# Right sides and split weights at chosen distances modulo 512 bytes, and the last norm's root on ScalarE, in a float32 network of six sub-layers

## The chip, the core and the metric

The kernel runs on one core of a Trainium2 chip. A core has a TensorE (PE, for matrix products, with its weight load shown as PEld), a VectorE (DVE), a ScalarE (ACT), a GpSimd (POOL) and a SyncE (SP, which here only issues DMAs), 128 partitions of on-chip memory that the engines read and write, and eight PSUM banks that PE writes its sums to. The metric is the device time of one execution in microseconds (us); single instructions are told in nanoseconds (ns).

## The reference

One sequence of 256 tokens of width 1024 passes two layers of three sub-layers each, all in float32. Each sub-layer normalises, scales and shifts its input by vectors made from a condition `c`, and adds a gated result to `x`:

```python
h = modulate(x, 0)                      # rms_norm(x) * (1 + scale) + shift
x = x + 0.5 * (1 + gate0) * ((silu(h @ w_gate) * (h @ w_up)) @ w_down)
h = modulate(x, 1)
y = hybrid_mixer(h, ...) if layer % 2 == 0 else mlstm_block(h, ...)
x = x + (1 + gate1) * y
h = modulate(x, 2)
x = x + 0.5 * (1 + gate2) * swiglu(h, ...)
...
return rms_norm(x, final_norm_g)
```

The order is feed-forward, hybrid (a gated linear recurrence beside a state-space mixer), feed-forward, feed-forward, mLSTM, feed-forward: sub-layers 0 to 5. The feed-forward hidden width is 2816, that is 22 blocks of 128. Nearly all work is in the projections, 2,928 weight blocks of 128 x 128.

## The kernel before, in words

**Products in parts.** The kernel keeps activations transposed, channels on partitions and the 256 tokens along the free side. A float32 product is made of three products of the fast type float32r: a number is split into a high part (rounded) and a low part (the rest), and high x high, low of the right side x high weights, and high x low weights are summed. Lines 312 to 314 (`multiply`) are these three matmuls of 256 columns; `project` runs them over the k blocks. In the interleaved starts of sub-layers 1 to 5 (`begin`, lines 359 to 361) four banks are filled in turn by matmuls of 258 columns, the last two columns being the shift. In the out projections of the feed-forward sub-layers and of the mLSTM (`out_project`, lines 413 and 415) the right side's high and low part lie behind each other, so one matmul of 512 columns with the high weights and one of 256 with the low weights do the same: a pair. Eight output chunks `d` of 22 (feed-forward) or 16 (mLSTM) pairs each make an out projection. Its result is added to `x` with the gate by DVE (line 420, once for each of the two sums of a pair), squared by ACT (line 296) and the squares are summed by DVE (line 300) for the next norm.

**Weights.** They come in the order of use, in 366 pieces of eight blocks, 512 KB each: SP's queue loads a piece into one of three raw buffers `wraw`, ACT copies the rounded high part `whi` (line 94), DVE subtracts it to give the low part `wlo` (line 95); each has six buffers. Pieces are made up to four ahead of use. Vectors from `c` (`ada`, line 209) are further loads and DVE operations between the pieces.

**Addresses.** Every tile takes a stretch of each partition, in the order in which the pools hand them out. Modulo 512 bytes the tiles that matmuls read lie as follows. The normalised input `hb` has rows of 640 numbers, the high part at their start and the low part 272 numbers (1,088 bytes) on, at 416 and 480. A part buffer is 1,024 + 16 numbers (4,160 bytes), each 64 further than the one before: the six of `whi` at 416, 480, 32, 96, 160, 224, those of `wlo` at 288, 352, 416, 480, 32, 96. The out projection's right sides are at 480 (`ph` of sub-layers 2 and 5; `ysb` and `ylb` of the hybrid), 0 (`ph` of sub-layers 0 and 3; half of the mLSTM's `yb`) or 32 (its other half), `xlb` of the hybrid at 64; in these the low part is 1,024 bytes behind the high one and so at the same place. Pieces named later lie so: 104 and 110 at 160 (`whi`) and 32 (`wlo`), 116 likewise, 167 at 416 and 480, 168 and 330 at 32 and 288.

**The end.** `rs_tokens` (called at line 1051) sums the squares over channels with four one-column matmuls (line 273, block by block: both summands of the first 128 tokens, then both of the second), and DVE makes the inverse root by a bit trick and three Newton steps (lines 278, 255 to 262; twelve operations). PE transposes `x`, already scaled by ACT with the norm's weights (line 1054), into four banks; ACT and DVE each scale two of 512 columns by the inverse root (lines 1062, 1064) and send each off (line 1065).

The compiler of the language puts the instructions of each engine in order by the data they need; nothing in the source fixes it but a few hints (`issue_after`, `add_manual_dep`).

## Time and profile before

| what | us |
|---|---|
| median of 3 runs (1157.63, 1157.66, 1162.23) | 1157.66 |
| the profiled execution | 1161.48 |
| its span, first to last instruction | 1159.6 |
| PE busy, of the span | 1135.5 |
| DVE busy | 958.6 |
| ACT busy | 640.1 |

The stages, by the first and last matmul of each in us of the span: feed-forward 0 from 22 (its `gu` matmuls) over 143 (out projection) to 204; hybrid to 396; feed-forward 2 to 588, its out projection from 526; feed-forward 3 to 777, its out projection from 714; mLSTM to 960, its out projection from 914; feed-forward 5 to 1151, its out projection from 1087.

A row of the timeline has start, length, engine, line, operation and the tiles that it writes and reads (`gu<-hb,whi`: into bank `gu`, from `hb` with the weights `whi`; buffer numbers are left out), then the shape. A matmul's length is modelled and overlaps the next one, so its pace is read from start to start. `xN` counts instructions. A bracket at the end is the engine's idle time before, and what ended it.

### The profile page before, as it was taken

What the parts mean: (1) busy time and instruction counts of PE and PEld (TensorE: products, weight loads), DVE (VectorE), ACT (ScalarE), POOL (GpSimd) and SP (SyncE); (2) the same over time, 40 slices, a digit from 0 to 9 for tenths busy, and PEclk for the clock granted to TensorE, in tenths of its full rate; (3) what the DMA queues carried; (4) which work ended last, traced back from release to release, by engine and by line L of the source; (5) the groups of instructions that cost most, each with busy time, mean ns of one, the idle gap of its engine ahead of it and who ended that gap; (6) DMA issues with size and microseconds to landing.
All of it is one profiled execution on the core that took longest, in us unless ns stands there. A gap on an engine that the chain in (4) does not pass through costs nothing.

```text
span 1159.6 us, 21861 instructions
## 1 busy us (share of the span) xinstructions
PE 1135.5 (98%) x8526; PEld 1080.9 (93%) x8526; DVE 958.6 (83%) x1838; ACT 640.1 (55%) x1070; POOL 8.8 (1%) x24
## 2 busy tenths in 40 slices
PE   7999999999998999999999999999999999999997
PEld 6999988999988999998899998889999889999986
DVE  7989999999888798788788888989869988666553
ACT  4465444778975564444454445448765366544451
POOL 0000000000000000000000000010000000000000
PEclk9999999999999999999999999999999999999999
DMA  8989989556555659888849799973532475775551
GB/s 321 344 299 362 369 301 323 200 184 203 175 182 164 189 191 325 298 313 301 269 148 323 279 344 346 329 266 99 158 110 73 133 241 157 253 229 188 183 182 37
DMA packets 74985, 272.25 MB, mean 235 GB/s; under 512 B 8417, under 2 KB 8577, under 8 KB 74882
## 3 DMA queue, kind: packets, MB, share of 16 engines
q1 hardware_dynamic: 74016, 268.99, 68.4%
q8 instruction: 67, 1.10, 0.4%
q0 software_dynamic: 432, 1.10, 0.3%
q10 hardware_dynamic: 434, 0.76, 0.2%
q14 instruction: 36, 0.29, 0.1%
HBM read 269.77 MB, written 1.05 MB: 234 GB/s over the span
## 4 chain that ended last, share of the span: by engine, by line
PE 83%; DVE 9%; DMA 4%; ACT 3%; issue 1%; ACTq 0%; DVEq 0%; SPq 0%
PE od L413 16%; PE gu L313 12%; PE gu L312 12%; PE gu L314 12%; PE od L415 8%; DMA wraw<-in_wst_dram 4%; DVE wlo L95 3%; ACT whi L94 1%; PE gu_f L361 1%; PE gu_f L359 1%; PE up L314 1%; PE up L313 1%; PE gu_f L360 1%; PE up L312 1%; DVE ada L209 1%
## 5 line engine op out<-in xcount | busy, mean ns | idle before, releaser
L94 ACT CAST whi<-wraw 128x1024 fp32r<-128x1024 f32 x364 | 380.3, 1047 | 299.0 <-DMA wraw<-in_wst_dram 164.1
L95 DVE TENSOR_TENSOR wlo<-wraw,whi 128x1024 fp32r<-128x1024 f32 x366 | 446.6, 1221 | 103.2 <-ACT whi L94 102.4
L313 PE MATMUL gu<-hb,whi 128*128 128x256 f32 x1312 | 369.3, 282 | 0.1
L314 PE MATMUL gu<-hb,wlo 128*128 128x256 f32 x1312 | 368.2, 282 | 0.0
L312 PE MATMUL gu<-hb,whi 128*128 128x256 f32 x1312 | 364.9, 282 | 1.5 <-ACT hb L328 1.5
L314 PEld LDWEIGHTS gu<-hb,wlo 128*128 128x128 f32 x1312 | 249.3, 190 | 0.0
L313 PEld LDWEIGHTS gu<-hb,whi 128*128 128x128 f32 x1312 | 248.1, 189 | 0.3 <-DVE hb L329 0.3
L312 PEld LDWEIGHTS gu<-hb,whi 128*128 128x128 f32 x1312 | 246.5, 190 | 2.0 <-ACT hb L328 1.8
L413 PE MATMUL od<-ph,whi 128*128 128x512 f32 x704 | 245.9, 394 | 1.6 <-DVE ph L306 1.6
L415 PE MATMUL od<-ph,wlo 128*128 128x256 f32 x704 | 196.6, 279 | 0.0
L209 DVE SCALAR_TENSOR_TENSOR ada<-ada,cact 128x1024 f32<-128x1024 f32 x144 | 174.9, 1218 | 0.0
L413 PEld LDWEIGHTS od<-ph,whi 128*128 128x128 f32 x704 | 132.2, 188 | 32.4 <-DVE ph L306 1.9
L415 PEld LDWEIGHTS od<-ph,wlo 128*128 128x128 f32 x704 | 132.2, 188 | 0.0
L305 ACT CAST ph<-fg 128x256 fp32r<-128x256 f32 x88 | 35.2, 406 | 91.3 <-DVE fg L440 91.0
L420 DVE SCALAR_TENSOR_TENSOR x<-od,gate,x 128x256 f32<-128x256 f32 x88 | 42.0, 480 | 25.6 <-PE od L415 19.5
L306 DVE TENSOR_TENSOR ph<-fg,ph 128x256 fp32r<-128x256 f32 x88 | 36.6, 421 | 13.1 <-ACT ph L305 13.1
L413 PE MATMUL od<-yb,whi 128*128 128x512 f32 x128 | 45.1, 396 | 0.0
L439 ACT ACTIVATE fg<-gu 128x256 f32<-128x256 f32 x82 | 30.7, 378 | 14.0 <-PE gu L314 14.0
L312 PE MATMUL zz<-hb,whi 128*128 128x256 f32 x128 | 37.6, 293 | 0.0
L314 PE MATMUL zz<-hb,wlo 128*128 128x256 f32 x128 | 37.2, 291 | 0.0
L313 PE MATMUL zz<-hb,whi 128*128 128x256 f32 x128 | 37.0, 289 | 0.0
L415 PE MATMUL od<-yb,wlo 128*128 128x256 f32 x128 | 35.9, 282 | 0.0
(398 smaller groups left out, 1869.3 us busy)
## 6 DMA issues: line engine op xcount, KB each, us to landing
wraw<-in_wst_dram SPq DMA_DIRECT2D x366, 512.0 KB, 4.5
ada<-in_adaT_dram SPq DMA_DIRECT2D x144, 512.0 KB, 5.4
xn<-in_x_dram SPq DMA_DIRECT2D x2, 512.0 KB, 4.0
wgr<-in_ml_wg_dram POOLq DMA_DIRECT2D x3, 256.0 KB, 6.1
out_dram<-res ACTq DMA_DIRECT2D x2, 256.0 KB, 3.0
out_dram<-res SPq DMA_DIRECT2D x2, 256.0 KB, 3.0
cols<-in_cols_dram ACTq DMA_DIRECT2D x1, 226.0 KB, 4.9
wkr<-in_ml_wkr_dram POOLq DMA_DIRECT2D x1, 128.0 KB, 2.5
```

The source lines that it names most:

```text
L94: raw_hi = nc.scalar.copy(hi, raw)
L95: self.last = nc.vector.tensor_tensor(out=lo, in0=raw, in1=hi.bitcast(F32), op=ALU.subtract)
L209: nc.vector.scalar_tensor_tensor(out=raw, in0=raw, scalar=1.0, in1=cact, op0=ALU.mult, op1=ALU.mult, accum_out=mods[s][:, m:m + 1])
L305: nc.scalar.copy(hi, src)
L306: nc.vector.tensor_tensor(out=both[:, 1, :], in0=src, in1=hi.bitcast(F32), op=ALU.subtract)
L312: m = nc.tensor.matmul(dst, wh, both[:, 0, :], start=start, stop=False, skip_group_check=True)
L313: nc.tensor.matmul(dst, wh, both[:, 1, :], start=False, stop=False, skip_group_check=True)
L314: nc.tensor.matmul(dst, wl, both[:, 0, :], start=False, stop=stop, skip_group_check=True)
L413: nc.tensor.matmul(bank, wh, both.rearrange("p i t -> p (i t)"), start=(k == 0), stop=False, skip_group_check=True)
L415: nc.tensor.matmul(sums[0], wl, both[:, 0, :], start=False, stop=(k == len(rhs) - 1), skip_group_check=True)
L420: nc.vector.scalar_tensor_tensor(out=xs_t[d], in0=part, scalar=g[:, d:d + 1], in1=xs_t[d], op0=ALU.mult, op1=ALU.add)
L439: nc.scalar.activation(g, b[:, 0:T], AF.Silu)
```

## The change

**Addresses.** `hb`'s rows become 768 numbers, with the low part 384 numbers (1,536 bytes) behind the high one, so both are alike modulo 512. `whi` loses its 16 spare numbers and `wlo` gets 128, so all six buffers of each lie alike; in the pieces of the feed-forward and mLSTM out projections (`WIDE`) the low part begins 16 numbers (64 bytes) into its buffer. Small unused tiles (`xpad`, `pad0` to `pad5`) take up space so that the following tiles land where wanted; the mLSTM's two halves get a size that is a multiple of 512 bytes. The scratch that the runtime keeps for POOL's DMAs goes from 16 to 8 KB a partition, which makes room. Modulo 512 the tiles now lie at: `hb` 448 (both parts), `whi` 128, `wlo` 128, or 192 in wide pieces, `ph` of all sub-layers and `yb` 192, `ysb` and `ylb` 448, `xlb` 32.

Right side less weights, modulo 512, is then 320 in every 256-column matmul on `hb`, `ysb` and `ylb`, for high and low weights alike; 64 (high) and 0 (low) in the pairs; 416 on `xlb` (16 blocks).

**The norms' sums.** The summing matmuls (now `sum_tokens`) take both token blocks of the first summand and then both of the second, under one start per bank.

**The end.** The last chunk of the last out projection uses `project`, one sum of 256 columns, and one update by DVE. A small root on ACT behind the square of chunk 5 brings the root's table in; the last norm's root is ACT's, followed on DVE by a reciprocal and one Newton step; the outputs leave in three pieces for each block of 128 tokens (256, 256 and 512 columns).

```diff
+WIDE = []
+for _i, _n in enumerate((ND * NF, 0, ND * NF, ND * NF, ND * 16, ND * NF)):
+    _e = sum(SUB_TILES[:_i + 1])
+    WIDE.append(((_e - _n) // PIECE, _e // PIECE))
-LO_ROW = 272
+LO_ROW = 384
...
-        hi = self.part_pool.tile([P, w + 16], F32R, tag="whi", name=f"whi{i}")[:, 0:w]
-        lo = self.part_pool.tile([P, w + 16], F32R, tag="wlo", name=f"wlo{i}")[:, 0:w]
+        o = 16 if any(p <= i < q for p, q in WIDE) else 0
+        hi = self.part_pool.tile([P, w], F32R, tag="whi", name=f"whi{i}")
+        lo = self.part_pool.tile([P, w + 128], F32R, tag="wlo", name=f"wlo{i}")[:, o:o + w]
...
-    hb = xp.tile([P, ND, 640], F32R, name="hb")
+    hb = xp.tile([P, ND, 2 * LO_ROW], F32R, name="hb")
+    xp.tile([P, 48], F32, name="xpad")
...
+            for i, q in enumerate(acc):
+                for b in range(2):
+                    m = nc.tensor.matmul(pt[:, b:b + 1], q[:, b * P:(b + 1) * P], ones[:, 0:1],
+                                         start=(i == b == 0), stop=(i == len(acc) - 1), skip_group_check=True)
...
+            elif s == 5 and d == ND - 1:
+                sums = [mm_bank(f"od{s}_{d}")[:, 0:T]]
+                project(sums[0], rhs)
...
+            elif d == 5:
+                root = small.tile([P, 1], F32, tag="root", name="root", bufs=1)
+                with tc.issue_after(last_act[0]):
+                    nc.scalar.activation(root, eps, AF.Sqrt)
...
-        half = [sp.tile([P, 2048 + 2056], F32, tag=f"half{i}", name=f"half{i}") for i in range(2)]
+        half = [sp.tile([P, 4224], F32, tag=f"half{i}", name=f"half{i}")[:, 0:2048 + 2056] for i in range(2)]
...
+                fp.tile([P, 56 if s in (2, 5) else 48], F32, name=f"pad{s}", bufs=1)
...
-    rs = rs_tokens(acc, D, "fin", "mm")
+    pt = sum_tokens(acc, "fin", "mm")
...
+    nc.scalar.activation(rs, pt[:, 0:2], AF.Sqrt, bias=eps, scale=1.0 / D)
+    nc.vector.tensor_scalar(out=v, in0=pt[:, 0:2], scalar1=1.0 / D, scalar2=EPS, op0=ALU.mult, op1=ALU.add)
+    nc.vector.reciprocal(rs, rs)
+    nc.vector.tensor_tensor(out=w, in0=rs, in1=rs, op=ALU.mult)
+    nc.vector.scalar_tensor_tensor(out=w, in0=w, scalar=-0.5, in1=v, op0=ALU.mult, op1=ALU.mult)
+    nc.vector.scalar_tensor_tensor(out=rs, in0=w, scalar=1.5, in1=rs, op0=ALU.add, op1=ALU.mult)
...
+    for lo, hi in ((0, 256), (256, 512), (512, 1024)):
+        for b in range(2):
...
-    nc = bacc.Bacc("TRN2", target_bir_lowering=False, num_devices=1)
+    nc = bacc.Bacc("TRN2", target_bir_lowering=False, num_devices=1, dynamic_dma_scratch_size=8192)
```

The order of instructions hardly moves outside the end. On PE, the last chunk of the last out projection, before (`od_7` is its bank, `ph` a right side, `rst_fin` the bank of the squares' sum):

```order
L413 MATMUL od_7_13764<-ph_20_13234,whi_13719 128x512
L415 MATMUL od_7_13764<-ph_20_13234,wlo_13720 128x256
L413 MATMUL od_7_13764<-ph_21_13301,whi_13719 128x512
L415 MATMUL od_7_13764<-ph_21_13301,wlo_13720 128x256
L273 MATMUL rst_fin<-ones,ssq_13304 128x1
L1056 MATMUL fin_13838<-ident,x 128x128
```

and now:

```order
L333 MATMUL od_7_13775<-ph_20_13243,whi_13730 128x256
L334 MATMUL od_7_13775<-ph_20_13243,whi_13730 128x256
L335 MATMUL od_7_13775<-ph_20_13243,wlo_13731 128x256
L333 MATMUL od_7_13775<-ph_21_13310,whi_13730 128x256
L334 MATMUL od_7_13775<-ph_21_13310,whi_13730 128x256
L335 MATMUL od_7_13775<-ph_21_13310,wlo_13731 128x256
L285 MATMUL rst_fin<-ones,ssq_13313 128x1 x2
L1098 MATMUL fin_13864<-ident,x 128x128
```

A pair has become a triple, and both sums of `ssq` stand ahead of the transposes (`fin`). The sums of the last square stood behind fourteen transposes with a second sum of `ssq` between them, and two transposes followed; now they stand, two in a row, behind nine transposes and ahead of seven.

On DVE, from the last update of `x` on, before (after the last row shown two more rounds of lines 260 to 262 follow, then the outputs):

```order
L420 SCALAR_TENSOR_TENSOR x<-od_7_13764,gate_13368,x 128x256 x2
L278 TENSOR_SCALAR rsv_fin<-rst_fin 128x2
L255 TENSOR_SCALAR rsw_fin<-rsv_fin 128x2
L257 TENSOR_SCALAR rsy_fin<-rsw_fin 128x2
L260 TENSOR_TENSOR rsw_fin<-rsy_fin 128x2
L261 SCALAR_TENSOR_TENSOR rsw_fin<-rsw_fin,rsv_fin 128x2
L262 SCALAR_TENSOR_TENSOR rsy_fin<-rsw_fin,rsy_fin 128x2
```

and now:

```order
L445 SCALAR_TENSOR_TENSOR x<-od_7_13775,gate_13377,x 128x256
L1089 TENSOR_SCALAR rsv_fin<-rst_fin 128x2
L1090 RECIPROCAL rsy_fin<-rsy_fin 128x2
L1091 TENSOR_TENSOR rsw_fin<-rsy_fin 128x2
L1092 SCALAR_TENSOR_TENSOR rsw_fin<-rsw_fin,rsv_fin 128x2
L1093 SCALAR_TENSOR_TENSOR rsy_fin<-rsw_fin,rsy_fin 128x2
L1106 TENSOR_SCALAR res<-fin_13865,rsy_fin 128x256 x2
L1106 TENSOR_SCALAR res<-fin_13867,rsy_fin 128x512
```

The reciprocal waits for ACT's root. On ACT, from the square of chunk 5 on, now (before, the table load, the two roots of `root` and `rsy_fin` and the third piece are not there):

```order
L316 ACTIVATE sq_o_5_13714<-x 128x256
L455 ACT_TABLE_LOAD
L455 ACTIVATE root<-eps 128x1
L1096 ACTIVATE x<-x,cols 128x256
L316 ACTIVATE sq_o_6_13772<-x 128x256
L1096 ACTIVATE x<-x,cols 128x256
L316 ACTIVATE sq_o_7_13843<-x 128x256
L1096 ACTIVATE x<-x,cols 128x256
L1088 ACTIVATE rsy_fin<-rst_fin,eps 128x2
L1104 ACTIVATE res<-fin_13864,rsy_fin 128x256 x2
```

No second table load follows, so square, copy and root run from one table.

43 lines of the change are left out of this document (26 added, 17 removed).

## Prediction

> **What bounds the kernel now.** I read the page's busy shares first, then the busy time of each engine by stage, then the waits, then the matmuls one by one in the timeline. The page's first part, with busy us, share of the span and instructions:
>
> ```profile
> PE 1135.5 (98%) x8526; PEld 1080.9 (93%) x8526; DVE 958.6 (83%) x1838; ACT 640.1 (55%) x1070; POOL 8.8 (1%) x24
> ```
>
> TensorE is nearly never idle. The next rows are stretches of the span: length, busy time and instruction count of PE, PEld, DVE, ACT and POOL, then granted clock, DMA share and GB/s. The first is `gu` of sub-layer 0, the second the hybrid, the third `gu` of sub-layer 2, the fourth its out projection, the last `gu` of sub-layer 5.
>
> ```profile
> 22.40:142.90 120.50, 120.50 (x1019) 120.50 (x1018) 112.30 (x186) 59.94 (x90) 0.00 (x0) 1.00 0.95 346
> 224.40:395.60 171.20, 165.14 (x1335) 157.31 (x1334) 149.62 (x325) 130.74 (x257) 0.00 (x0) 0.99 0.57 178
> 415.70:526.00 110.30, 110.18 (x929) 109.85 (x928) 91.23 (x138) 55.98 (x84) 0.00 (x0) 1.00 0.88 300
> 526.00:587.50 61.50, 61.50 (x356) 53.75 (x355) 49.20 (x76) 28.82 (x39) 1.06 (x2) 1.00 0.84 276
> 980.60:1087.30 106.70, 106.70 (x902) 106.70 (x901) 70.21 (x95) 50.99 (x75) 0.00 (x0) 1.00 0.69 218
> ```
>
> In the feed-forward stages PE is busy throughout at full clock, and everything else has room, least of it DVE in sub-layer 0 (112.3 of 120.5 us). Supply of weights is ahead there: the waits (us in total, times, longest) show ACT's high parts waiting for matmuls to give buffers back, which only a producer that is ahead does. Most of its DMA waits are of the same kind, since a transfer starts when a raw buffer comes free.
>
> ```profile
> ACT whi L94 <- DMA wraw<-in_wst_dram: 164.1, 124, 4.7
> ACT whi L94 <- PE od L413: 53.9, 38, 1.8
> ACT whi L94 <- PE gu L313: 27.0, 19, 1.7
> ```
>
> So the pace is how close one matmul starts behind the other. In `gu`, 110.30 us over 929 matmuls are 118.7 ns each, 106.70 over 902 are 118.3; I use 118.4. An out projection's 176 pairs (512 columns, then 256) take 61.50 us, 349.4 ns a pair. The question is whether addresses set these numbers. Call distance the right side's address less the address of weights loaded beside it, modulo 512 bytes; the allocation in the section on the kernel gives it. The timeline (start, length) of sub-layer 2's out projection, first with piece 167, whose high part lies at distance 64 and low part at 0, then with piece 168, at 448 and 192:
>
> ```profile
> 534.41 0.39 PE L413 MATMUL od<-ph,whi 128*128 128x512 f32 x1
> 534.63 0.28 PE L415 MATMUL od<-ph,wlo 128*128 128x256 f32 x1
> ...
> 537.13 0.39 PE L413 MATMUL od<-ph,whi 128*128 128x512 f32 x1
> ...
> 537.47 0.40 PE L413 MATMUL od<-ph,whi 128*128 128x512 f32 x1
> 537.71 0.28 PE L415 MATMUL od<-ph,wlo 128*128 128x256 f32 x1
> ...
> 540.30 0.39 PE L413 MATMUL od<-ph,whi 128*128 128x512 f32 x1
> ```
>
> From the first to the last of each group are eight pairs: 2.72 us or 340.0 ns a pair, against 2.83 us or 353.8. Same instructions, same stage; only addresses differ. Single starts inside the first group lie 0.22 and 0.12 apart, so about 227 and 113. Now 256-column matmuls, in the hybrid's out projection, with a high part at distance 320 and a low part at 448:
>
> ```profile
> 365.05 0.28 PE L312 MATMUL od<-ysb,whi 128*128 128x256 f32 x1
> 365.17 0.28 PE L313 MATMUL od<-ysb,whi 128*128 128x256 f32 x1
> ...
> 367.43 0.28 PE L312 MATMUL od<-ysb,whi 128*128 128x256 f32 x1
> ```
>
> These are 21 matmuls in 2.38 us, 113.3 ns each. But the same tile, with another piece at the same distances, earlier:
>
> ```profile
> 348.47 0.28 PE L312 MATMUL od<-ysb,whi 128*128 128x256 f32 x1
> ...
> 350.13 0.28 PE L314 MATMUL od<-ysb,wlo 128*128 128x256 f32 x1
> ```
>
> Fourteen in 1.66 us are 118.6 each. A third piece at 320 and 448 is back at the faster pace (12 in 1.36 us, 113.3):
>
> ```profile
> 388.33 0.28 PE L312 MATMUL od<-ylb,whi 128*128 128x256 f32 x1
> ...
> 389.69 0.28 PE L312 MATMUL od<-ylb,whi 128*128 128x256 f32 x1
> ```
>
> So 256-column matmuls have two rhythms, in step (113.3) and out of step (118 to 119), and distance 320 allows the first without forcing it. The out projection's 64 and 0 held 340 through the whole stretch.
>
> **The change part by part.** *Out projections.* Every one of the wide pieces now has distances 64 and 0, those of the 340 ns stretch. There are 810 pairs (176 in three sub-layers, 128 in the mLSTM, 154 in the last, whose eighth chunk is rewritten). At 349.4 less 340.0 that is 9.4 ns x 810 = 7.6 us, all on the path, since PE is never idle there (61.50 of 61.50). I take 7, as a new piece may cost a beat; the bounds are 0 (the gain hangs on something else than distance) and 7.6.
>
> *The 256-column stages.* All three matmuls of a k step now have distance 320. `gu` has 1312 x 3 = 3,936 of them; in step they gain 118.4 - 113.3 = 5.1 ns, together 20.1 us. I take 17.7, as if one in eight still ran out of step after a break. Upper bound 20.1, lower 0 (out of step all the time), or less, below. The remaining users of the normalised input and of the hybrid's results are 480 matmuls of the interleaved starts, 1,488 in the hybrid and the mLSTM, and 384 of the hybrid's out projection: 2,352 x 4.5 ns is 10.6 us. In the hybrid, though, DVE has 149.6 and ACT 130.7 of 171.2 us and PE waits for them at times, so a faster matmul partly buys a longer wait: I take 5, between 0 and 10.6.
>
> For the weights' own road a faster PE asks for 1,016 matmuls x 113.3 = 115.1 us in the first `gu` stage, where DVE's work is 112.3 us: 98% full, with 362 GB/s of DMA where 346 are shown. Just enough if nothing is lost. The cover of the buffers that wait for PE in the rows above shrinks, but stays.
>
> [...]
>
> *The end.* The rows from the last chunk's update to the output:
>
> ```profile
> 1148.89 1.00 DVE L420 SCALAR_TENSOR_TENSOR x<-od,gate,x 128x256 f32<-128x256 f32 x2 [5.69 <-PE od L415]
> 1149.93 0.42 ACT L296 ACTIVATE sq_o<-x 128x256 f32<-128x256 f32 x1 [6.64 <-DVE x L420]
> 1150.39 0.38 PE L273 MATMUL rst_fin<-ones,sq_o 128*128 128x1 f32 x2
> 1150.64 0.36 PE L273 MATMUL rst_fin<-ones,ssq 128*128 128x1 f32 x2
> 1150.86 0.36 PE L273 MATMUL rst_fin<-ones,sq_o 128*128 128x1 f32 x2
> 1151.26 0.16 DVE L278 TENSOR_SCALAR rsv_fin<-rst_fin 128x2 f32<-128x2 f32 x1 [1.37 <-PE rst_fin L273]
> ...
> 1153.43 0.16 DVE L262 SCALAR_TENSOR_TENSOR rsy_fin<-rsw_fin,rsy_fin 128x2 f32<-128x2 f32 x1
> 1153.62 1.41 DVE L1064 TENSOR_SCALAR res<-fin,rsy_fin 128x512 f32<-128x512 f32 x2
> ```
>
> One update of the last chunk instead of two saves 0.50. Its 22 pairs become triples of 256 columns: 340 ns in step (no cost), 3 x 118.4 out of step (+0.1 us over today's pairs). Summing both blocks of the running sum early leaves two matmuls behind the last square, not three: -0.22. The 12 small operations from 1151.26 to 1153.62 (2.36 us, 0.2 a step) become a root on ACT, a handover and four on DVE. For ACT the nearest small operation, and for the reciprocal the same operation elsewhere, are:
>
> ```profile
> L590 ACT ACTIVATE hv<-hv x1: 215/215/215, 208.6 to 208.6; 128x16 f32<-128x16 f32 x1
> L975 DVE RECIPROCAL mlr<-mlr x2: 167/172/178, 878.6 to 903.1; 128x4 f32<-128x4 f32 x2
> ```
>
> 0.22 + 0.1 + 4 x 0.2 = 1.1, so -1.2. Three output pieces per side instead of two add about one fixed start, +0.15 and another issue. Seven transposes that now stand behind the last sum on PE run beside the root. Sum -1.7, between -2.2 and 0 (if the third store ends later by as much as the root saves). The table load for the root is put behind the square of chunk 5; the nearest load, and ACT's idle time before a late square, are
>
> ```profile
> 348.80 1.28 ACT L775 ACT_TABLE_LOAD   x1
> 1142.32 0.42 ACT L296 ACTIVATE sq_o<-x 128x256 f32<-128x256 f32 x1 [6.08 <-DVE x L420]
> ```
>
> so 1.28 us vanish in 6.08; without that cover they would eat three quarters of the end's gain.
>
> *The rest at nothing.* The order of the two-column sums ahead of five norms moves single columns by a few matmuls in a stream that PE runs through. The halved scratch concerns POOL's own transfers; the largest and POOL's waits are
>
> ```profile
> wgr<-in_ml_wg_dram POOLq DMA_DIRECT2D x3, 256.0 KB, 6.1
> POOL wgr L798 <- DVE wg L801: 59.9, 2, 49.0
> ```
>
> If the smaller scratch made each of the three wait for the one before, 6 us would be added to a chain that today waits 59.9 for DVE; the cover is the half sub-layer before the mLSTM needs them. One constant on POOL at the start is hidden by the first loads.
>
> **Sum.** 7 + 17.7 + 5 + 1.7 = 31.4 us. The profiled execution took 1161.48 us (span 1159.6), 3.8 over the median of the runs; the terms are matmul pitches, the same in either, so 1157.66 - 31.4 = 1126.
>
> **The rivals.** *Out of step.* The hidden state matters more than the distance: 348.47 to 350.13 shows 118.6 at the very distances that gave 113.3 later. Once every distance is alike nothing jolts the stream out of a bad rhythm either. For it: that stretch. Against: of the three stretches at 320 and 448 two were in step. Then out projections and end give 7 + 1.7, the tighter rhythm about 1 more: 1148; mixtures lie between 1126 and 1148.
>
> *Addresses don't matter, or not these.* All weights of before lie at 32 modulo 64, all of after at 0 modulo 64, and no row shows the second. If the good stretches hang on that, or on neighbours in time, only the end is left: 1156. [...] The pairs of 340.0 and 353.8 ns speak against it.
>
> *Slower: a bad rhythm made permanent.* The worst stretch of `gu`, piece 330, with distances 384 and 192:
>
> ```profile
> 1047.37 0.28 PE L312 MATMUL gu<-hb,whi 128*128 128x256 f32 x1
> ...
> 1050.27 0.28 PE L312 MATMUL gu<-hb,whi 128*128 128x256 f32 x1
> ```
>
> 24 matmuls in 2.90 us, 120.8 each. If aligned weights at distance 320 lock into that, 2.4 ns x (3,936 + 2,352) is +15.1; with pairs at 353.8 in the out projections +3.6; less 1.7: 1175. It turns slower once the 256-column pitch exceeds 118.4 by 8.7/6,288 = 1.4 ns with the pairs improved.
>
> *Supply becomes the bound.* If DVE can't go above its 93% of the first `gu` stage, the stage keeps 120.5 us and 1,016 x 5.1 = 5.2 us are lost: 1131.
>
> **How the numbers follow.** In step 0.50 (1126, 1117 to 1133); supply-bound 0.06 (1131); out of step or mixed 0.31 (1133 to 1150); nothing from addresses 0.08 (1156); slower 0.05 (1175). The low end takes every upper bound: 7.6 + 20.1 + 10.6 + 2.2 = 40.5, so 1117. The high end is 1150, out of step with a smaller gain at the end; 0.13 is left above it. 0.5%, 5.8 us, is about what a measurement of this kernel can tell from no change. Faster by more (below 1151.9): the first three cases, 0.87; same 0.08; slower 0.05.
>
> **What would show it.** In the new timeline: out projection pairs at 340 ns in all five stages, not only where a piece happens to fit; `gu` at 113 to 114 ns a matmul, its stages 101 to 103 us instead of 106.7; PE busy share unchanged at 98%; the norm's end 1.7 us shorter. I am wrong if `gu` still runs at 118 with constant distances (rhythm, not distance), if the pairs are not 340 (alignment), or if DVE and DMA waits of PE appear in sub-layer 0.

## The result, and the profile after

The changed kernel took 1147.04 us (median of 5 runs, 1142.78 to 1149.60) against 1157.66 for the kernel before (5 runs, 1156.84 to 1162.23): a ratio of 0.9895, 95% interval 0.9865 to 0.9926. So it is faster, by about a third of the 31.4 us that were forecast. Its profiled execution took 1148.33 us, with a span of 1146.6 against 1159.6.

The page's first part shows an engine that is as busy as before, over a shorter span:

```profile
PE 1124.3 (98%) x8548; PEld 1072.7 (94%) x8548; DVE 957.8 (84%) x1831; ACT 642.6 (56%) x1074; POOL 8.6 (1%) x25
```

The stretches of the span, in the columns that the prediction explains: the out projection of sub-layer 0, `gu` of sub-layer 0, the hybrid, `gu` of sub-layer 2, its out projection, `gu` of sub-layer 5.

```profile
141.40:202.80 61.40, 61.40 (x353) 53.82 (x352) 56.21 (x85) 30.35 (x40) 1.53 (x3) 1.00 0.89 311
...
22.40:141.20 118.80, 118.80 (x1011) 118.80 (x1010) 112.74 (x186) 59.71 (x90) 0.00 (x0) 1.00 0.96 350
224.40:391.00 166.60, 162.57 (x1332) 154.76 (x1332) 149.32 (x324) 130.68 (x256) 0.00 (x0) 1.00 0.58 182
411.00:520.30 109.30, 109.18 (x925) 108.80 (x925) 90.75 (x137) 55.84 (x84) 0.00 (x0) 1.00 0.88 302
...
520.60:580.20 59.60, 59.60 (x352) 52.88 (x352) 49.03 (x76) 28.85 (x38) 1.07 (x2) 1.00 0.86 283
974.00:1077.60 103.60, 103.60 (x882) 103.60 (x881) 68.45 (x92) 49.37 (x74) 0.00 (x0) 1.00 0.69 221
```

`gu` is hardly quicker: 109.30 us over 925 matmuls are 118.2 ns, 103.60 over 882 are 117.5; before they were 118.7 and 118.3. From its first matmul to its last, the out projection of sub-layer 2 fell from 61.2 to 59.7 us; the one of sub-layer 0, with the same instructions at the same distances, did not (61.3 before, 61.5 now). Single matmuls show why. First `gu` in sub-layer 2 (24 matmuls from the first to the last row), then eight pairs in sub-layer 2 and eight in sub-layer 0:

```profile
470.00 0.28 PE L333 MATMUL gu<-hb,whi 128*128 128x256 f32 x1
...
472.83 0.28 PE L333 MATMUL gu<-hb,whi 128*128 128x256 f32 x1
...
549.78 0.39 PE L438 MATMUL od<-ph,whi 128*128 128x512 f32 x1
...
552.50 0.39 PE L438 MATMUL od<-ph,whi 128*128 128x512 f32 x1
...
169.71 0.40 PE L438 MATMUL od<-ph,whi 128*128 128x512 f32 x1
...
172.51 0.40 PE L438 MATMUL od<-ph,whi 128*128 128x512 f32 x1
```

2.83 us over 24 are 117.9 ns a matmul, out of step. 2.72 over 8 are 340.0 ns a pair, 2.80 are 350.0. I call three 256-column matmuls of one k step a triple from here on: in step it takes 340 ns, out of step 353, so that triples and pairs are told in the same unit. Over the whole trace the mean `gu` triple fell from 355.6 to 353.3 ns, and what had varied between about 350 and 365 from piece to piece now stands at 353 or 354, but for the first piece of sub-layer 5 (340). Before the change no `gu` triple, from its start to the next one's, was below 346. The pairs stand at 340.1 in sub-layers 2, 3 and 5, at 350.0 in 0 and, for the most part, in 4.

The waits still show weights ahead of their use, as before:

```profile
ACT whi L101 <- DMA wraw<-in_wst_dram: 164.8, 128, 2.9
...
ACT whi L101 <- PE od L438: 50.3, 38, 1.7
ACT whi L101 <- PE gu L334: 26.6, 16, 3.0
```

The end, from the last chunk's update on:

```profile
1138.09 0.48 DVE L445 SCALAR_TENSOR_TENSOR x<-od,gate,x 128x256 f32<-128x256 f32 x1 [5.86 <-PE od L335]
...
1138.60 0.42 ACT L316 ACTIVATE sq_o<-x 128x256 f32<-128x256 f32 x1 [6.29 <-DVE x L445]
...
1139.80 0.26 ACT L1088 ACTIVATE rsy_fin<-rst_fin,eps 128x2 f32<-128x2 f32 x1 [0.24 <-PE rst_fin L285]
1140.10 0.16 DVE L1089 TENSOR_SCALAR rsv_fin<-rst_fin 128x2 f32<-128x2 f32 x1 [1.53 <-ACT rsy_fin L1088]
...
1140.95 1.53 DVE L1106 TENSOR_SCALAR res<-fin,rsy_fin 128x256 f32<-128x256 f32 x3
```

From the start of that update to the end of the span it is 8.5 us (1146.6 - 1138.09) where it was 10.7 (1159.6 - 1148.89).

Where the 13.0 us of span went, from the first matmuls of the stages and the last ones of the out projections in both timelines (a stage before less the same stage after):

| stage | gain, us | forecast |
|---|---|---|
| the four `gu` stages with their starts (1.6, 0.7, 0.8, 1.2) | 4.3 | 17.7 and a part of the 5 |
| hybrid and mLSTM (3.5, -0.2) | 3.3 | the rest of the 5 |
| five out projections (-0.2, 1.5, 0.8, 0.0, 1.3) | 3.4 | 7 |
| the end | 2.2 | 1.7 |

(0.1 us went the other way ahead of the first stage.) Of the hybrid's 3.5 us up to 1.7 may be the clock's and not the change's: in the execution profiled before, the clock granted to PE was at half speed for 3.4 us from 375.8 on, and in this one at full speed all through the hybrid.

### The profile page after: what moved, and what is told of

Its sections match the earlier page's. It is cut to its first block, busy times and chain, and to the rows that moved or that the text cites. A ratio compares the mean times of both kernels' runs of the same rounds, so it can differ in the third digit from the quotient of the medians.

```text
span 1146.6 us, 21903 instructions
## 1 busy us (share of the span) xinstructions
PE 1124.3 (98%) x8548; PEld 1072.7 (94%) x8548; DVE 957.8 (84%) x1831; ACT 642.6 (56%) x1074; POOL 8.6 (1%) x25
## 4 chain that ended last, share of the span: by engine, by line
PE 84%; DVE 8%; DMA 4%; ACT 2%; issue 1%; ACTq 0%; DVEq 0%; SPq 0%
PE od L438 13%; PE gu L335 13%; PE gu L334 13%; PE gu L333 13%; PE od L440 7%; DMA wraw<-in_wst_dram 4%; DVE wlo L102 3%; ACT whi L101 1%; PE gu_f L380 1%; PE gu_f L382 1%; PE up L335 1%; PE up L334 1%; PE up L333 1%; PE gu_f L381 1%; PE od L333 1%
## 5 line engine op out<-in xcount | busy, mean ns | idle before, releaser
L335 PEld LDWEIGHTS gu<-hb,wlo 128*128 128x128 f32 x1312 | 246.8, 188 | 0.0
L438 PE MATMUL od<-ph,whi 128*128 128x512 f32 x682 | 234.0, 391 | 2.4 <-DVE ph L327 2.4
L440 PE MATMUL od<-ph,wlo 128*128 128x256 f32 x682 | 189.0, 277 | 0.0
L438 PEld LDWEIGHTS od<-ph,whi 128*128 128x128 f32 x682 | 128.1, 188 | 29.6 <-DVE ph L327 2.7
L440 PEld LDWEIGHTS od<-ph,wlo 128*128 128x128 f32 x682 | 128.0, 188 | 0.0
```

The lines of the kernel that those rows point to most:

```text
L335: nc.tensor.matmul(dst, wl, both[:, 0, :], start=False, stop=stop, skip_group_check=True)
L438: nc.tensor.matmul(bank, wh, both.rearrange("p i t -> p (i t)"), start=(k == 0), stop=False, skip_group_check=True)
L440: nc.tensor.matmul(sums[0], wl, both[:, 0, :], start=False, stop=(k == len(rhs) - 1), skip_group_check=True)
```

## The experiments

Each kernel differs from the changed one unless it says otherwise. Times are medians, and ratios are to the kernel before on the same chip; in brackets stand the range of the runs and the 95% interval of the ratio.

**The changed kernel once more.** Theory R: at one and the same distance there are two rhythms. Theory D: distance alone sets the pace. Nothing is edited.

> The changed kernel once more, unchanged. Theory R (two rhythms): at one and the same distance a stream of matmuls can run in step or out of step, and what a stage happens to enter with decides; then sub-layers 0 and 4, whose pairs ran at 350 ns in the first profile, and 2, 3 and 5, which ran at 340, need not be the same ones here, and the runs scatter by some us (a stage of 176 pairs is worth 1.8 us, a stage of gate and up products 4 us). Theory D (distance alone): the same sub-layers at the same pace to the ns, and runs within 0.3%. Both: 1143 to 1150 us.

1145.35 us (6 runs, 1143.31 to 1150.75), ratio 0.9881 (0.9853 to 0.9909). The timeline of sub-layer 0's out projection, eight pairs, to be held against the rows at 169.71 and 172.51 above:

```profile
169.76 0.39 PE L438 MATMUL od<-ph,whi 128*128 128x512 f32 x1
...
172.48 0.39 PE L438 MATMUL od<-ph,whi 128*128 128x512 f32 x1
```

2.72 us, 340.0 ns a pair, where the same program took 350.0 in its other profiled execution. All five out projections ran at 340 here; `gu` stayed at 353.3. Nothing in the program differs between these two, only the execution (and perhaps the chip: that of the first isn't on record). Within the first execution alone the same distances already gave both paces, in different sub-layers. That falls against D.

**Only the end.** The edit is all of the change to sums and end; parts and rows are as before.

```diff
-LO_ROW = 384
+LO_ROW = 272
...
-        hi = self.part_pool.tile([P, w], F32R, tag="whi", name=f"whi{i}")
-        lo = self.part_pool.tile([P, w + 128], F32R, tag="wlo", name=f"wlo{i}")[:, o:o + w]
+        hi = self.part_pool.tile([P, w + 16], F32R, tag="whi", name=f"whi{i}")[:, 0:w]
+        lo = self.part_pool.tile([P, w + 16], F32R, tag="wlo", name=f"wlo{i}")[:, 0:w]
...
-    hb = xp.tile([P, ND, 2 * LO_ROW], F32R, name="hb")
+    hb = xp.tile([P, ND, 640], F32R, name="hb")
```

> The end and the norms' sums as changed, all distances as before (every tile 64 bytes further, so differences are kept). Both theories: pairs at 349 and triples at 355.6 ns on average as before, and 1.7 us from the end, ratio 0.9985. If the end or the sums' order brought most of the 10.6 us, about 0.991.

1159.23 us (12 runs, 1157.31 to 1162.52), ratio 0.9989 (0.9972 to 1.0006). Triples at 355.6 and pairs at 348.6 to 349.4, as before. The runs bound what the end gives at 3.2 us, of some 14, so most of the gain of the change comes with the addresses. The start of the last update in this trace:

```profile
1149.29 0.48 DVE L444 SCALAR_TENSOR_TENSOR x<-od,gate,x 128x256 f32<-128x256 f32 x1 [5.87 <-PE od L334]
```

From there to the end of the span (1157.8) it is 8.5 us, as in the changed kernel.

**Low parts of the wide pieces not moved** (distance 64 for both parts of a pair).

```diff
-        o = 16 if any(p <= i < q for p, q in WIDE) else 0
+        o = 0
```

> The changed kernel without the shift of the low weights in the out projections: pairs at distances 64 and 64 instead of 64 and 0. Theory D: the pairs lose what 0 gave, 347 to 350 ns in all five out projections, 810 x 8 ns less what sub-layers 0 and 4 had not gained, so 4 to 5 us slower than the changed kernel. Theory R: 64 and 64 may also have an in-step rhythm at 340; then no difference beyond the scatter of the runs.

1154.49 us (12 runs, 1150.78 to 1160.22), ratio 0.9949 (0.9931 to 0.9968). In the profile (of the slowest of these runs) every out projection ran at 349 to 353 ns a pair, none at 340; `gu` at 353.3 as in the changed kernel. 0.9949 less 0.9881 is 0.7%, 8 us: without this distance more than half of what the change gained is gone.

**Low part of `hb` 64 bytes off**, so that high and low part no longer lie alike.

```diff
-LO_ROW = 384
+LO_ROW = 272
...
-    hb = xp.tile([P, ND, 2 * LO_ROW], F32R, name="hb")
+    hb = xp.tile([P, ND, 768], F32R, name="hb")
```

> The changed kernel with the low part of the normalised input 64 bytes off again (distances 320 from the high part; 384 from the low part to the low weights), the pairs untouched. Theory D: triples leave 353.3 ns for the mixed values of before (353.4 where 320 met 384, before), so under 1 us. Theory R: with unlike distances inside a triple no stretch in step can hold, but hardly any did in the changed kernel either: within 1 us, and no triple at 340.

1153.24 us (12 runs, 1149.54 to 1158.65), ratio 0.9946 (0.9927 to 0.9966). Both theories had said within 1 us of the changed kernel, and it lost 8. (The 384 of the text above is the low part's distance to the high weights, which it meets.) `gu` stood at 353.3 as before the edit; held against the changed kernel's trace above, 7 of the 8 us were lost in the out projections, which had not been edited: 350.0 ns a pair in sub-layers 0, 2 and 5, 341 in 3 and 4. So 64/0 allows the pace of 340 and doesn't secure it. How a stage that is left alone comes to another rhythm was not found out; I take from it that what runs ahead of a stage may have a say in it; no run shows that.

**Two sweeps.** Every two pieces of `gu` (from the 17th piece on in sub-layer 0) and every single piece of the out projections get other distances, 64 of them in random order; one pool of the mLSTM has 3 buffers instead of 4 for room, here and in all later kernels that move high parts.

```diff
+_all = [(16 * (c // 8), 16 * (c % 8)) for c in range(64)]
...
+    SHIFT[_p] = SHIFT[_p + 1] = _all[_c]
...
-        o = 16 if any(p <= i < q for p, q in WIDE) else 0
+        oh, ol = SHIFT[i]
```

> A map: high and low weights of each piece are shifted by 0 to 448 bytes in steps of 64, each on its own, 64 pairs of shifts in a random order; every two pieces of gate and up products and every single piece of the out projections have another. (One buffer less in the mLSTM, to make room.) Read from the trace: the pace of the last triples or pairs of each piece. Theory D: the pace is a function of the two distances, some of which give 340, and the same in both maps. Theory R: each pair of distances gives one of a few fixed paces (340, 350 to 354, more), and which one also hangs on the piece before, so the two maps, with different orders, disagree for some pairs; 320 and 320 at 353 in both, 64 and 0 at 340 for pairs in one at least.

> The same map in another random order. As for the first: theory D, the same pace for the same distances within 1 ns; theory R, disagreement for some, where one map has 340 and the other 350 or more.

1156.87 and 1153.94 us (one run each). Median ns of a triple by distance, first sweep/second sweep, a part of the table that the timelines give:

```
high \ low   0         64        192       256       320       448
0            360/360   353/353   353/353   360/360   353/353   353/353
192          353/353   340/340   340/353   353/367   340/340   340/340
256          360/360   353/353   353/353   360/360   353/353   353/353
320          349/349   340/340   360/340   353/349   340,353   360/340
448          353/353   340/340   353/340   353/353   340/340   340/353
```

The paces are a few fixed values, and neither sweep makes a smooth function of them. The entry for 320/320 stands for the many pieces that were left there; the hybrid's out projection, which was not edited, ran at 340 in over a third of its triples in either sweep. At 256/0 it is 360 each time; at 320/64, 192/320, 448/64 and 448/320 it was 340 each time; at the changed kernel's 320/320 it was both. I concluded that 320/320 was the wrong choice and 320/64 the right one. The next runs showed that to be wrong.

**The best distances of the sweeps**, for triples, for pairs and for both, and the slowest for triples. The edits, in this order:

```diff
-        o = 16 if any(p <= i < q for p, q in WIDE) else 0
+        o = 16 if any(p <= i < q for p, q in WIDE) else 64
...
+        o = 80 if any(p <= i < q for p, q in WIDE) else 0
...
+        o = 80 if any(p <= i < q for p, q in WIDE) else 64
...
+        oh, ol = (0, 16) if any(p <= i < q for p, q in WIDE) else (16, 80)
```

> The changed kernel with one number different: in the pieces that feed 256-column matmuls the low part lies 256 bytes further on, so that its distance is 64 where the changed kernel has 320. High parts, normalised input and the out projections' pairs are as in the changed kernel. Theory R (a stretch settles in one of a few fixed rhythms; some distances allow only the fast one, 320/320 allows two): the map of the sweeps shows 340 ns at 320/64 in every sample, so gu runs at 340 ns a triple from its first piece to its last, and 1,312 triples x 13.3 ns = 17.5 us go; of the 806 other triples (10.7 us if all gain the same) between half and all: 1119 to 1124 us. Theory N (340 in the sweeps came from the jolt of a new distance at every second piece; where every piece has the same, a stream settles at 353 whatever it is): 1145 to 1148 us, gu at 353. Theory S (supply binds once the matmuls are faster): gu of sub-layer 0 stays near 118 ns a matmul with waits of PE for DVE, the other gu stages at 113; about 1125 to 1129.

> The changed kernel with one number different: in the out projections' pieces the low part's distance is 256 where the changed kernel has 0 (high part 64 as there). The triples are as in the changed kernel. Theory R: the map shows 340 ns a pair in every sample at 64/256, but 350 or 340 at 64/0, so now all five stages run at 340 in every run; the gu stages stay at 353. Against the changed kernel this takes away the slow out projections that some of its runs have (up to 9.5 ns x 480 pairs = 4.6 us in a run with three such stages) and so most of the scatter: 1143 to 1146 us, its runs within about 3 us of each other. Theory N: pairs at 350 in some stages as before, 1145 to 1149, same scatter as the changed kernel.

> Both of the above: triples at 320/64, pairs at 64/256. Theory R: gu at 340 ns a triple and all five out projections at 340 ns a pair, in every run: 1117 to 1122 us, the runs within about 3 us. That is the forecast for the changed kernel (1126) met by other distances. Theory N: 1143 to 1148. Theory S: 1123 to 1127, with waits of PE in gu of sub-layer 0.

> The changed kernel with the triples' pieces at the distances that were slowest in every sample of the map, 256 for the high part and 0 for the low part, all parts still at multiples of 64 bytes; pairs as in the changed kernel; to make room the mLSTM's pool of row buffers has 3 instead of 4. Theory R: 360 ns a triple from end to end, 6.7 ns x 1,312 = 8.8 us in gu and up to 5.4 in the others: 1153 to 1161 us, so at or above the kernel before. Theory N (a steady stream is at 353 whatever the distance): 1145 to 1149.

1147.80 us (ratio 0.9903, 0.9881 to 0.9925), 1149.71 (0.9915, 0.9892 to 0.9938), 1150.09 (0.9918, 0.9898 to 0.9939), each of 6 runs, where theory R had said 1119 to 1124, 1143 to 1146 and 1117 to 1122: none is told apart from the changed kernel. The slow distances gave 1155.24 (12 runs; 0.9961, 0.9947 to 0.9975), as theory R had it. `gu` of sub-layer 2 in the timeline, 24 matmuls each, first at 320/64, then at 256/0:

```profile
469.88 0.28 PE L333 MATMUL gu<-hb,whi 128*128 128x256 f32 x1
...
472.71 0.28 PE L333 MATMUL gu<-hb,whi 128*128 128x256 f32 x1
```

```profile
470.02 0.28 PE L333 MATMUL gu<-hb,whi 128*128 128x256 f32 x1
...
472.90 0.28 PE L333 MATMUL gu<-hb,whi 128*128 128x256 f32 x1
```

117.9 and 120.0 ns. So 320/64, which ran at 113.3 in every sample of the sweeps, runs at 117.9 from one end to the other when every piece has it; and the pairs at 64/256 were at 350 in two stages of one of these kernels. My theory as it stood fell: neither of the two distances that were tried throughout for triples, and neither of the two for pairs, forces the fast rhythm. Distances say which rhythms there are (at 256/0 only the one of 360); something else chooses among them. In the sweeps each piece had come from another distance. That gave theory K: both rhythms keep themselves up, and a jolt, such as a change of distance, can throw a stream from one into the other.

**Distances in turn.** Two pieces each; first 320/64 and 192/320, then 192/320, 448/64, 64/320, 448/320.

```diff
-        o = 16 if any(p <= i < q for p, q in WIDE) else 0
+        oh, ol = (0, 16) if any(p <= i < q for p, q in WIDE) else [(0, 64), (32, 0)][i // 2 % 2]
...
+        oh, ol = (0, 16) if any(p <= i < q for p, q in WIDE) else [(32, 0), (96, 64), (64, 0), (96, 0)][i // 2 % 4]
```

> The changed kernel, but in the pieces that feed 256-column matmuls the distances (high part, low part) alternate, two pieces 320/64, two pieces 192/320. Out projections as in the changed kernel; the mLSTM's pool of row buffers has 3 instead of 4, as in the run with slow distances. Theory K (340 and 353 ns a triple both keep themselves up at 320/64 and at 320/320; which one a stream has is decided where it is interrupted, and a change of distance can be such a kick: in the sweeps 192/320 was entered three times from 349 to 354 ns and ran at 340 each time, 320/64 once from 353 and once from 340): gu runs at 340 from its first or second change of distance on, 17.5 us less than the changed kernel if it holds through, half of that if each change to 320/64 throws it out again: 1121 to 1139 us. Theory F (320/64 with constant neighbours showed that a long stream ends at 353; what the sweeps showed was luck of each slot's entry): 1144 to 1152, gu at 353 to 356.

> As the run with two alternating distances, but with four in turn, two pieces each: 192/320, 448/64, 64/320, 448/320. Every one of them ran at 340 in all samples of the sweeps, 64/320 entered from 448/64 and 448/320 entered from 64/320 among them. Theory K: gu at 340 ns a triple but for a triple or two at a change, every stage; 1121 to 1127 us, and PE then waits a little in sub-layer 0, where the weights' road is nearly full. Theory F: 1144 to 1152.

1138.49 us (6 runs, 1137.06 to 1145.76), ratio 0.9823 (0.9790 to 0.9856), and 1139.41 (6 runs, 1132.97 to 1144.63), 0.9819 (0.9786 to 0.9852). `gu` of sub-layer 0 and a stretch of `gu` in sub-layer 2, of the second kernel:

```profile
22.00:137.00 115.00, 115.00 (x1012) 114.77 (x1011) 110.02 (x183) 59.91 (x90) 0.00 (x0) 1.00 0.97 351
...
428.00:510.00 82.00, 82.00 (x726) 82.00 (x725) 68.91 (x101) 41.85 (x63) 0.00 (x0) 1.00 0.92 321
```

82.00 us over 726 are 112.9 ns (records at both edges counted), in step; the mean `gu` triple is 340.6 and 340.3 in the two. K, and not F. But the four distances should have given 1121 to 1127: each `gu` stage is 4 us shorter, and the total by less. I come back to that.

**One kick.** Does the alternation hold the stream in step, or does one jolt do? In the first kernel all pieces keep the changed kernel's 320/320, but for two in each feed-forward sub-layer at 192/320; in the second they keep 320/64.

```diff
+KICK = {_first[_s] + _a + _b for _s, _a in ((0, 16), (2, 8), (3, 8), (5, 8)) for _b in (0, 1)}
...
-        o = 16 if any(p <= i < q for p, q in WIDE) else 0
+        oh, ol = (0, 16) if any(p <= i < q for p, q in WIDE) else (32, 0) if i in KICK else (0, 0)
```

> The changed kernel with its own distances, 320/320 for the triples and 64/0 for the pairs, except for two pieces (16 triples) in each of the four feed-forward sub-layers, which stand at 192/320: the 17th and 18th piece of sub-layer 0, the 9th and 10th of sub-layers 2, 3 and 5. The mLSTM's pool of row buffers has 3 instead of 4. Theory K (both rhythms keep themselves up, a jolt decides which one a stream has): from those 16 triples to the end of its stage, gu runs at 340 ns although its distances are again those at which the changed kernel runs at 353; 1,024 + 64 triples x 13.3 ns = 14.5 us less than the changed kernel, given back up to 4 us in sub-layer 3, where the products for the out projection came late in both kick runs: 1131 to 1137 us. Theory A (it is the alternation that holds 340; constant distances drift back to 353): only the 64 triples gain, 0.9 us: 1144 to 1150 us. Between them, if 192/320 to 320/320 throws the stream out in some stages: 1137 to 1144.

> As the run with one kick in each sub-layer, but with 320/64 instead of 320/320 around the kicks. That distance ran at 353 from end to end without a kick. Theory K: 340 from the kick to the end of each stage, 1131 to 1137 us; the change from 192/320 to 320/64 kept 340 each time that both pieces were uninterrupted in the run with two alternating distances, so this one is the surer of the two. Theory A: 1144 to 1150.

1137.82 us (5 runs, 1136.36 to 1142.41), ratio 0.9823 (0.9807 to 0.9840), and 1140.21 (5 runs, 1135.77 to 1143.43), 0.9835 (0.9812 to 0.9858). The first kernel's timeline in sub-layer 2; the two pieces of the kick begin at 417.55:

```profile
414.73 0.28 PE L335 MATMUL gu<-hb,whi 128*128 128x256 f32 x1
...
417.55 0.28 PE L335 MATMUL gu<-hb,whi 128*128 128x256 f32 x1
...
418.61 0.28 PE L335 MATMUL gu<-hb,whi 128*128 128x256 f32 x1
...
419.29 0.28 PE L335 MATMUL gu<-hb,whi 128*128 128x256 f32 x1
...
470.29 0.28 PE L335 MATMUL gu<-hb,whi 128*128 128x256 f32 x1
...
472.67 0.28 PE L335 MATMUL gu<-hb,whi 128*128 128x256 f32 x1
```

24 matmuls in 2.82 us ahead of it (117.5 ns); three triples later 6 in 0.68 (113.3); and 50 us on, long back at 320/320, 21 in 2.38 (113.3). In all four stages the stream stays in step from the kick to the out projection, and so it does in the second kernel: each of the eight kicks turns 353 into 340 ns, after three triples at most. The same distance, the same instructions, both paces: `gu` missed its gain because it ran in the slow one of two rhythms that 320/320 allows, and that is shown.

Two things are not shown. The totals, 1137.8 and 1140.2 us, lie above the 1131 to 1137 that K gave; more on that below. And what it is in a kick that works stays open: all of these go to 192/320, which ran at 340 in every sample of the sweeps, and no kernel has 192/320 throughout. Not every change of distance does it: of 117 changes in the two sweeps that met `gu` out of step, 17 brought it into step, and the kernel before has one at every piece with none of its `gu` triples in step.

**Kicks for the pairs as well** (64/256 and 448/256 in turn, beside the four distances of the triples).

```diff
+        oh, ol = [(0, 80), (32, 80)][i // 2 % 2] if any(p <= i < q for p, q in WIDE) else [(32, 0), (96, 64), (64, 0), (96, 0)][i // 2 % 4]
```

> The run with four distances in turn, and the out projections' pairs kicked as well, two pieces at 64/256 and two at 448/256. The question is the scatter of the runs (1133 to 1145 us with the four distances). Theory K for pairs too: their stages fall out of step in some runs only (up to 9.5 ns x 810 = 7.7 us), a kick every two pieces ends that, so all five at 340 and the median at 1131 to 1135 with a scatter below 6 us. Otherwise (the scatter comes from elsewhere, or pairs don't answer to kicks): 1137 to 1143, scatter as before.

1136.85 us (6 runs, 1132.89 to 1143.79), ratio 0.9821 (0.9797 to 0.9845). All five out projections were in step (340.0 to 342.2 ns), and this trace is of the slowest run, 1143.79 us; the scatter is 10.9 us as before. So in the kicked kernels it is not the pairs' rhythm. Against the trace with four distances, the fastest run there and in step as well, its span is 10.8 us longer: 4.2 in the hybrid and 3.3 in the start of sub-layer 3. In the slow trace the granted clock is at half speed in both places, for 6.8 us from 369.1 on and for 3.4 us from 580.7 on; in the fast one it is at half speed in neither. Part of the scatter is clock, then.

**Where the rest goes.** The largest of PE's waits in the kernel with one kick (5.9 us in two pieces, the longer one 3.5), and two stretches of sub-layer 3's out projection around it (the granted clock is the third number from the end):

```profile
PE od L440 <- DVE ph L329: 5.9, 2, 3.5
```

```profile
705.00:709.40 4.40, 0.62 (x2) 0.30 (x2) 4.40 (x8) 2.75 (x5) 0.00 (x0) 1.00 0.88 321
709.40:716.20 6.80, 5.37 (x17) 4.60 (x18) 5.63 (x8) 3.47 (x4) 0.00 (x0) 0.50 1.00 380
```

The changed kernel waits 2.4 us there, at full clock. From its first matmul to its last, this out projection takes 70.1 us here (1.7 of them because its pairs stand at 350 ns) and 67.2 in the kernel with four distances, against 62.4 in the changed kernel. That is more than `gu` of sub-layer 3 had gained (3.8 and 4.2 us). The last two kernels leave sub-layer 3 without a kick (in the second, at 320/320), and all else as with one kick and with four distances.

```diff
-KICK = {_first[_s] + _a + _b for _s, _a in ((0, 16), (2, 8), (3, 8), (5, 8)) for _b in (0, 1)}
+KICK = {_first[_s] + _a + _b for _s, _a in ((0, 16), (2, 8), (5, 8)) for _b in (0, 1)}
...
-        oh, ol = (0, 16) if any(p <= i < q for p, q in WIDE) else [(32, 0), (96, 64), (64, 0), (96, 0)][i // 2 % 4]
+        oh, ol = (0, 16) if any(p <= i < q for p, q in WIDE) else (0, 0) if _first[3] <= i < _first[4] else [(32, 0), (96, 64), (64, 0), (96, 0)][i // 2 % 4]
```

> The run with one kick in each feed-forward sub-layer, without the one in sub-layer 3, so that gu there stays at 353 ns (280 triples x 13.3 = 3.7 us given up). Theory G (the gain of sub-layer 3 is given back behind it: DVE has the conditioning's sums to do beside its products, the last products reach the out projection 4.0 to 5.9 us late where the changed kernel waits 1.8 to 2.4, and the granted clock falls to 0.5 to 0.7 for some us after that wait): the wait is back at about 2 us, the clock stays at 1.00, and the median is the same or up to 3 us better: 1135 to 1139 us against 1137.8. Theory H (the gain in gu is kept and the wait has another cause): 3.7 us slower, 1141 to 1142.

> The run with four distances in turn, with sub-layer 3's pieces left at 320/320. Theory G: the same or up to 3 us better than 1139.4, with runs closer together: 1135 to 1139 us, a wait of about 2 us at the start of sub-layer 3's out projection. Theory H: 1143.

1136.68 us (4 runs, 1134.07 to 1139.27), ratio 0.9803 (0.9780 to 0.9825), and 1135.81 (5 runs, 1132.24 to 1137.49), 0.9792 (0.9769 to 0.9815). The first one's wait at the same place, and the clock around it:

```profile
PE od L440 <- DVE ph L329: 0.6, 1, 0.6
```

```profile
702.00:707.00 5.00, 4.39 (x27) 3.63 (x26) 4.27 (x7) 2.64 (x4) 0.00 (x0) 1.00 1.00 383
707.00:712.00 5.00, 5.00 (x31) 4.41 (x31) 5.00 (x8) 2.11 (x2) 0.00 (x0) 1.00 0.98 299
```

`gu` of sub-layer 3 is 3.8 us longer, and the total no longer: theory G, not H. The out projection behind it takes 60.6 and 63.7 us. One point of G missed: in the second kernel a wait of 2.0 us is left, and the clock doesn't stay at 1.00 behind it. The likely reason is that the faster `gu` outruns DVE, which in that sub-layer has the condition's sums to do beside its products (in the kernel with four distances, from 571 to 705 us):

```profile
L102 DVE TENSOR_TENSOR wlo<-wraw,whi 128x1024 fp32r<-128x1024 f32 x45 | 54.9, 1223 | 5.7 <-ACT whi L101 5.6
L219 DVE SCALAR_TENSOR_TENSOR ada<-ada,cact 128x1024 f32<-128x1024 f32 x30 | 36.6, 1219 | 0.0
```

36.6 us of such sums, over a quarter of the stretch. No run moves these sums, so the reason rests on the waits: 4.0 to 5.9 us in the five traces with sub-layer 3 in step, 0.4 to 2.9 in eleven with `gu` there at 353 to 360 ns. A twelfth of these, the slowest run of the kernel without the moved low parts, waits 4.3 us at 353, so the pace of `gu` isn't all. The last of these kernels is the best of the study: 10 to 12 us faster than the changed kernel by the ratios (0.9792 against 0.9881 and 0.9895), with runs within 5.3 us. The two pairs of kernels with and without sub-layer 3 do not part by their medians (their intervals overlap); it is the waits and the clock that part them. The mean granted clock of a whole run is 0.991 to 0.993 (one kick, 5 runs) and 0.990 to 0.996 (four distances, 6 runs) with sub-layer 3 in step, 0.994 to 0.999 and 0.995 to 0.999 without.

## Why the prediction was wrong

**The step that failed** is the 256-column term: "All three matmuls of a k step now have distance 320. ... I take 17.7, as if one in eight still ran out of step after a break." In the changed kernel not one in eight but practically all of `gu` ran out of step, at 117.8 ns instead of 113.3, and the term gave 3.0 us (355.6 - 353.3 = 2.3 ns x 1,312 triples). The prediction had named this very sign ("if `gu` still runs at 118 with constant distances"). The price of being in step was about right: the kernel with one kick shows 113.3 ns at 320/320, and 13.3 ns a triple where the prediction had 15.3.

The frequency was wrong. The prediction had three stretches at 320 and 448, two of them in step, and read them as odds for each moment. But a rhythm mostly stays once it is there, so each stretch was a single draw, and three are few. Nor were they at the distance of the change: 320/320 stands in no row of the trace before, and the sweeps show that the low weights' distance counts as well (320 with 0, 64 and 256 gave 349, 340 and 353 or 349). In the changed kernel each stage began out of step or fell out of it after one piece, and nothing brought it back. The rival "Out of step" said so in one sentence ("nothing jolts the stream out of a bad rhythm either") and gave 1148; it got 0.31. That 1148 is 1 us from the measured 1147.04 is partly luck: its 7 us from the out projections were 3.4, and more than its 1 us came from the tighter rhythm and from the clock in the hybrid.

**Out projections.** The mechanism was right and the size depends on the run. 340 ns at 64/0 is real, and the kernel without that distance is 0.7% (8 us) slower, near the 7 us that I took. But 64/0 has a second rhythm of 350 ns, which sub-layers 0 and 4 had in the profiled execution: 3.4 us came there. The kernel with `hb`'s low part moved kept 64/0 and was as slow, with 350 in three stages. "Held 340 through the whole stretch" was again one draw of eight pairs.

**The other 256-column matmuls.** 5 forecast, from 4.5 ns a matmul, for which no row was given; 3.3 came in the hybrid and the mLSTM, from other sources than the one named: most of those triples stood at 353 too, the starts' 258-column triples fell from 364 to 357 ns, PE's idle time in the hybrid's stretch fell from 6.1 to 4.0 us, and up to 1.7 us are the half clock of the execution before.

**The end.** 1.7 forecast, 2.2 in the profile (10.7 to 8.5 us). The root went as worked out: 1139.80 to 1140.95 are 1.15 us for a forecast 1.1. The stores' term had the wrong sign: from the first scaled output to the span's end it is 5.65 us (1146.6 - 1140.95) where it was 5.98 (1159.6 - 1153.62), so the pieces save 0.3 instead of costing 0.15. The runs of the end alone bound it at -0.7 to +3.2 us, and can't tell the two numbers apart; their trace has the 8.5 us of the changed kernel.

**The rivals.** Addresses do matter (no 1156). The locked bad rhythm exists, at 256/0 and not here, with the price that was named (120.0 ns for 120.8). The supply rival had the right mechanism in the wrong place: in `gu` of sub-layer 0 DVE kept pace even in step (110.0 of 115.0 us, and PE busy throughout), but in sub-layer 3, where over a quarter of its time goes to the condition's sums, PE waits longer for its products and the gain is given back.

What stays open: what puts a stream into one rhythm or the other at a stage's start (two executions of one program differed), what it is in a kick that brings the stream into step, and what sets off the half clock in some executions of the kicked kernels and not in others.

## What to carry to other kernels

When a back-to-back stream shows two paces at the same addresses, look how long each lasts before reading odds out of it: few long stretches are few draws. Making conditions uniform removes the disturbances as well, so ask which state the uniform stream starts in; if it is the slow one, one deliberate irregularity of a kind that was seen to work can be worth more than perfect order (here 1137.82 us with one kick in each feed-forward sub-layer, against 1147.04 and 1145.35). And where a stage gets faster, look at its far end for what arrives late there now, and at the clock behind that wait.

## What the runs showed of the hardware

In the sweeps the triples of 256 columns ran at a few paces (340, 349, 353 and 360 ns, once 367, in the table above). Three were seen for hundreds of matmuls without change, all in `gu` of sub-layer 2: 340 with four distances (82.00 us over 726), 353 in the changed kernel (87.00 over 742, from 428 on) and 360 at 256/0 (87.00 over 727, from 428 on; records at both edges counted). Two paces were seen at one set of addresses: 353 and 340 at 320/320, 350 and 340 at 64/0. In step, a weight load starts 110 ns ahead of its matmul (the kernel before, from 365.05 on), at 353 ns a triple 115 or 116 ahead (the changed kernel, from 470.00 on). Which of the two sets the other isn't shown.

The weights' place counts in these traces: with the weights at another place (and one mLSTM pool smaller) `gu` goes from 353 to 360 ns, or from 117.9 to 120.0 ns a matmul in the rows above. What makes the distance count, no run shows.

Half clock was seen behind short waits. In these traces the granted clock is full or half, and but for the end of the span half lasts 3.4 us at a time (the kernel before, from 375.8 on), 6.8 (the kernel with one kick, from 709.4 on) or 10.2 (the kernel with kicks for the pairs as well, in sub-layer 3's out projection). In the kernel with one kick it came inside the second of two waits of 2.4 and 3.5 us, as the rows above show; the changed kernel's single wait of 2.4 us there left the clock at 1.00. But in the last kernel a single wait of 2.0 us, over at 707.92, was followed by half speed:

```profile
PE od L439 <- DVE ph L328: 2.0, 1, 2.0
```

```profile
708.60:712.00 3.40, 3.40 (x12) 2.90 (x11) 3.40 (x5) 2.10 (x2) 0.00 (x0) 0.50 0.78 243
```

So the length of the wait alone doesn't say whether the clock goes down.
